# Hybrid RWKV-7 / MLA block on one core: a group's transposes in two steps on other PSUM banks, and two matmul orders turned round

## The chip, the cores and the metric

The kernel runs on one core of a Trainium2 chip. The time is device microseconds (us) of one execution on that core, compared by the median of several runs. The engines are TensorE (PE, with its weight loads PEld), VectorE (DVE), ScalarE (ACT), GpSimd (POOL) and SyncE (SP), which issues the DMAs here.

## The reference, cut to what matters

One layer over 256 latent and 256 context tokens of width 2048, all in float32. A combined input projection feeds a bidirectional RWKV-7 branch (16 heads of 64, two directions), a latent attention branch and gates; the branches are projected, merged and added to the stream.

```python
def rwkv7_step(S, xs):
    r, w, k, v, kk, akk = xs
    sa = jnp.einsum("dbhij,dbhj->dbhi", S, -kk)
    S = S * w[..., None, :] + sa[..., :, None] * akk[..., None, :] + v[..., :, None] * k[..., None, :]
    return S, jnp.einsum("dbhij,dbhj->dbhi", S, r)
...
S_ctx, y_c = rwkv_scan(r_c, v_c, kk_c, dec_c, a_c, km_c, S0)
_, y_x = rwkv_scan(r_x, v_x, kk_x, dec_x, a_x, km_x, S_ctx)
...
x_new = x + g_x * merge_branches(o_rw_x, o_ml_x, mg_x, w_branch_rwkv[i], w_branch_mla[i], w_out[i])
```

The scan over tokens is what the changed functions work on: the kernel does it in chunks of 64 tokens, with the values `v` and the keys of a chunk as matmul operands.

## The kernel before, in words

**Three terms for one product.** Most products are made with float32 operands split into a high and a low part, both read in a faster matmul form: `wh`, `wl` of a weight (ACT copies `wh` from the loaded `w`, DVE subtracts it to get `wl`, by `parts_of`) and `hmh`, `hml` of the activations. `mm3` issues three matmuls: wh with hmh, wh with hml, wl with hmh. PE's rows name the moving operand first, so they read `acc<-hmh,wh`, `acc<-hml,wh`, `acc<-hmh,wl`.

**Fill.** `proj_g` and `branch_g` make such products in bursts of twelve matmuls of 256 columns, or six of 512 columns, into the PSUM tiles named `acc`. `E.burst` keeps a burst together: its first matmul (its head, line L117 in the profile) is placed by ordinary priority, and the rest (L120) follow it by a high priority and an added dependency. Nothing in the scan waits soon for most of these bursts, so they are the work that is put between the steps of the scan. Here they are called fill.

**Groups of two halves.** A half is one pair of heads with one of the two token sets. Group k holds the latent half of pair k-1 (m = 0) and the context half of pair k (m = 1); the first and the last group hold one half. Four stretches of work follow one another for a group:

- `front` makes the decays, keys and products of each half (`wk<-Qc,BK` for context, `wk<-QR,BK` for latent) and starts `diagonal`, which inverts small blocks: the products go through DRAM (`dl`, `ln`), 28 small DVE operations work on `wt`, and the inverse comes back through DRAM (`dw`) as `WT`.
- `front2` transposes the values (two 128x128 transposes for a half, `wk<-cc,cv`, copied into `UV`) and the keys (eight for a half, `wk<-cc,BK`, copied by ACT into `BKT`). Each half takes three steps, so a full group takes six, all with the two PSUM buffers named `wk`.
- `back` begins with four levels (`lev`), 32 small matmuls each for a full group, into the two PSUM buffers named `lv`. Level 0 reads `WT` and `AQ`; the next three read `Z` or `ZN` with `WT`, `TF` or `W`. After each level DVE makes the next operand (`Z<-lv`, `W<-WT,lv`), one instruction for each half. In each pair of matmuls the latent one comes first. A level is a burst with two heads (four in level 0).
- Then `back` walks four chunks with three products each: `chp<-UV,AQ`, `chp<-xs,W`, `chp<-UV,BKT` (with `chp<-QR,Mn` and `chp<-AR,UV` for the latent outputs), each followed by a DVE or ACT copy that the next one reads.

**What sets the order.** `drive` writes the instructions down in Python from generators: at every `yield` of a chain it may put bursts of fill in between, by a model of time of its own. Conditions such as `yield lambda: backs >= k` hold a chain back. `bg_v(p)` (a value projection) becomes ready when the counter `fronts` passes a number. Then the scheduler of the tile framework orders the instructions of each engine by priority and by its own idea of when operands are there. The engines work through these orders as written.

The stages in time: the first projections to about 135 us, the scan with its fill to about 890 us, attention with fill to about 1117 us, then the last projections without fill.

## Time and profile before

| | |
|---|---|
| three runs | 1257.06, 1259.44, 1263.16 us (median 1259.44) |
| the profiled execution | 1256.53 us, of which its span is 1254.7 us |
| PE busy, share of the span | 1189.0 us, 95% |
| PEld, DVE, ACT busy | 1000.5 us (80%), 937.7 us (75%), 596.4 us (48%) |
| mean granted TensorE clock | 0.993 |
| chain that ended last | PE 70%, DMA 15%, DVE 11%, ACT 2% |

The span is what the instructions cover; the 1.8 us more in the execution's own time lie around it. PE is the engine to look at: it is idle for 66 us of the span, and only that idle time, and gaps between matmuls that the record counts as busy, can be gained or lost without a change in the work itself.

### The profile page before, as it was taken

How to read it: one execution, taken by the hardware profiler on the slowest of the kernel's cores; microseconds unless marked ns; L12 is line 12 of the kernel's file. 1: busy time of each engine (PE TensorE's matmuls, PEld its weight loads, DVE VectorE, ACT ScalarE, POOL GpSimd, SP SyncE). 2: the span in 40 equal slices, each digit the busy share in tenths (PEclk: the TensorE clock that was granted, in tenths of full speed). 3: DMA queues.
4: the chain of work that ended last, by engine and by line, in shares of the span. 5: the costliest groups of instructions: out<-in, count | busy, mean ns of one | idle time of the engine just before them, and what ended most of it. 6: DMA issues, size and time to landing. Idle time of an engine off the chain costs nothing.

```text
span 1254.7 us, 30101 instructions
## 1 busy us (share of the span) xinstructions
PE 1189.0 (95%) x11613; PEld 1000.5 (80%) x11613; DVE 937.7 (75%) x2642; ACT 596.4 (48%) x1244; POOL 1.9 (0%) x9
## 2 busy tenths in 40 slices
PE   5999998998999999999999899899999999899998
PEld 2665787787877777878887789789899999899886
DVE  4444767868888788888998888865877777768655
ACT  3444542444453454434544456344565656535443
POOL 0000000000000000000000000000000000000000
PEclk9999899999999999999999999999999999999999
DMA  9999447655554455544662655444855433689774
GB/s 377 347 351 352 144 122 180 163 156 146 128 154 126 119 139 136 148 117 124 167 151 62 162 157 146 127 114 142 255 181 152 138 109 115 193 283 295 220 254 139
DMA packets 214127, 222.53 MB, mean 177 GB/s; under 512 B 113168, under 2 KB 138400, under 8 KB 213472
## 3 DMA queue, kind: packets, MB, share of 16 engines
q1 hardware_dynamic: 213984, 220.61, 59.1%
q8 instruction: 91, 1.49, 0.5%
q14 instruction: 52, 0.43, 0.1%
HBM read 201.52 MB, written 19.03 MB: 176 GB/s over the span
## 4 chain that ended last, share of the span: by engine, by line
PE 70%; DMA 15%; DVE 11%; issue 2%; ACT 2%; SPq 0%; DVEq 0%; ACTq 0%
PE acc L120 29%; PE chp L115 11%; PE lv L115 6%; PE acc L117 5%; DMA wm<-in_w_mod_ss 4%; PE a L115 4%; PE ch L115 3%; DMA w<-in_w_proj 3%; DVE wl L142 3%; PE wk L115 2%; PE wk L127 2%; DMA ln<-dl 2%; PE wk L120 2%; PE acc L115 1%; DVE wt L142 1%
## 5 line engine op out<-in xcount | busy, mean ns | idle before, releaser
L142 ACT CAST wh<-w 128x512 fp32r<-128x512 f32 (+1 forms) x484 | 291.0, 608 | 328.4 <-PE acc L120 128.5
L142 DVE TENSOR_TENSOR wl<-w,wh 128x512 fp32r<-128x512 f32 (+1 forms) x480 | 322.6, 675 | 149.6 <-ACT wh L142 77.4
L120 PE MATMUL acc<-hmh,wl 128*128 128x256 f32 (+1 forms) x1312 | 396.7, 302 | 3.9 <-DVE wl L142 3.7
L120 PE MATMUL acc<-hml,wh 128*128 128x256 f32 (+1 forms) x1312 | 394.7, 301 | 0.0
L120 PE MATMUL acc<-hmh,wh 128*128 128x256 f32 (+1 forms) x928 | 273.8, 295 | 0.0
L120 PEld LDWEIGHTS acc<-hmh,wl 128*128 128x128 f32 x1312 | 248.8, 190 | 18.0 <-DVE wl L142 7.0
L120 PEld LDWEIGHTS acc<-hml,wh 128*128 128x128 f32 x1312 | 249.5, 190 | 8.8 <-issue 1.0
L120 PEld LDWEIGHTS acc<-hmh,wh 128*128 128x128 f32 x928 | 176.2, 190 | 5.0
L117 PE MATMUL acc<-hmh,wh 128*128 128x256 f32 (+1 forms) x384 | 146.6, 382 | 7.0 <-DVE th L142 3.5
L117 PEld LDWEIGHTS acc<-hmh,wh 128*128 128x128 f32 x384 | 72.8, 190 | 33.1 <-issue 15.1
L142 DVE TENSOR_TENSOR pr<-wt 64x14 f32<-64x14 f32 (+6 forms) x224 | 42.5, 190 | 2.6
L142 DVE TENSOR_TENSOR wt<-wt,pr 64x14 f32<-64x14 f32 (+6 forms) x224 | 42.3, 189 | 2.2
L115 PE MATMUL a<-hmh,wh 128*128 128x512 f32 x96 | 41.2, 429 | 0.0
L115 PE MATMUL a<-hmh,wl 128*128 128x512 f32 x96 | 38.6, 402 | 0.4 <-DVE wl L142 0.4
L115 PE MATMUL pm<-wm,ssil 128*32 128x256 f32 x512 | 34.5, 386 | 4.4 <-DMA wm<-in_w_mod_ss 4.2
L115 PE MATMUL a<-hml,wh 128*128 128x512 f32 x96 | 38.4, 400 | 0.0
L115 PE MATMUL chp<-obh,wl 128*128 128x256 f32 x128 | 36.2, 283 | 0.0
L115 PE MATMUL chp<-obl,wh 128*128 128x256 f32 x128 | 36.2, 283 | 0.0
L115 PE MATMUL chp<-obh,wh 128*128 128x256 f32 x128 | 36.2, 283 | 0.0
L142 ACT ACTIVATE hx<-hx,mod 128x256 f32<-128x256 f32 x32 | 17.5, 594 | 37.8 <-DVE mod L142 37.8
L142 DVE TENSOR_TENSOR hml<-hx,hmh 128x512 fp32r<-128x512 f32 x16 | 11.1, 693 | 29.0 <-ACT hmh L142 29.0
L115 PEld LDWEIGHTS pm<-wm,ssil 128*32 128x32 f32 x512 | 13.4, 109 | 23.3 <-DMA wm<-in_w_mod_ss 11.5
(347 smaller groups left out, 2223.6 us busy)
## 6 DMA issues: line engine op xcount, KB each, us to landing
w<-in_w_proj SPq DMA_DIRECT2D x296, 256.0 KB, 3.1
wm<-in_w_mod_ss SPq DMA_DIRECT2D x64, 512.0 KB, 7.5
w<-in_w_mod_g SPq DMA_DIRECT2D x64, 256.0 KB, 3.4
w<-in_w_br SPq DMA_DIRECT2D x64, 256.0 KB, 3.9
w<-in_w_out SPq DMA_DIRECT2D x64, 256.0 KB, 3.5
WT<-dw SPq DMA_DIRECT2D x32, 256.0 KB, 4.8
w<-in_w_first SPq DMA_DIRECT2D x32, 192.0 KB, 4.9
thd<-th SPq DMA_DIRECT2D x48, 128.0 KB, 2.9
```

The costliest lines, as they stand in the source:

```text
L115: return self.engine.matmul(out, lhsT=lhsT, rhs=rhs, **kw)
L117: self.head.append(self.engine.matmul(out, lhsT=lhsT, rhs=rhs, **kw))
L120: i = self.engine.matmul(out, lhsT=lhsT, rhs=rhs, **kw)
L127: return self.engine.transpose(*a)
L142: return fn(out, *a, **kw)
```

## The change

Four edits in one:

- `front2` takes all halves of a group at once. The values of both are transposed into one `wk` buffer (four transposes), then the keys of the first half into two `lv` buffers (eight transposes); the copies into `UV` come after. A second step transposes the keys of the second half. It waits for the values of both pairs, and `fronts` is raised by two at the end.
- `mm3w` takes the place of `mm3` in `proj_g` and `branch_g`: wl with hmh first, then wh with hmh, then wh with hml.
- In `lev` the two matmuls of a pair change places: context (m = 1) first, then latent.
- The steps of `front2` are two for a full group instead of six, which moves where `drive` puts fill.

```diff
+    def mm3w(ps, ah, al, bh, bl, start, stop):
+        E.matmul(ps, lhsT=al, rhs=bh, start=start, stop=False)
+        E.matmul(ps, lhsT=ah, rhs=bh, start=False, stop=False)
+        E.matmul(ps, lhsT=ah, rhs=bl, start=False, stop=stop)
...
-                            mm3(ps[:, 0:n], wh[:, cs], wl[:, cs], hmh[:, kk, 0:n], hml[:, kk, 0:n], kk == 0, kk == KT - 1)
+                            mm3w(ps[:, 0:n], wh[:, cs], wl[:, cs], hmh[:, kk, 0:n], hml[:, kk, 0:n], kk == 0, kk == KT - 1)
...
-        def front2(h, m, UV):
...
+        def front2(hs_, UV):
             ps = wk()
+            for m, h in enumerate(hs_):
+                t0 = 0 if h % 2 else T
+                for i in range(2):
+                    c0 = T * m + 128 * i
+                    E.transpose(ps[:, c0:c0 + 128], cvs_[h // 2][:, t0 + 128 * i:t0 + 128 * i + 128], ident)
+            def keys(h):
+                Q, AQ, AR, BK = halves[h]
+                BKT = rw.tile([P, 8, P], F32, name="BKT", bufs=2)
+                for i in range(2):
+                    pt = lvp()
+                    for j in range(4):
+                        E.transpose(pt[:, 128 * j:128 * j + 128], BK[:, 4 * i + j].rearrange("p a t -> p (a t)"), ident)
+                    S.copy(BKT[:, 4 * i:4 * i + 4].rearrange("p a t -> p (a t)"), pt)
+                halves[h] = (Q, AQ, AR, BKT)
+            keys(hs_[0])
...
+                        copies[b](UV6[hss[1 - g], g, :, :, b], src)
             yield
+            for h in hs_[1:]:
+                keys(h)
                 yield
...
-                            for t, fn, out in zip(ps, fns, outs):
+                            for t, fn, out in list(zip(ps, fns, outs))[::-1]:
...
-                for m, h in enumerate(hs_):
-                    yield lambda: h // 2 in cvs_
-                    yield from front2(h, m, UV)
-                    fronts += 1
+                yield lambda: hs_[-1] // 2 in cvs_
+                yield from front2(hs_, UV)
+                fronts += len(hs_)
...
-                        mm3(ps[:, 0:T], wh[:, cs], wl[:, cs], *(t[:, 4 * i + k] for t in ob[0]), i + k == 0, i * 4 + k == 7)
+                        mm3w(ps[:, 0:T], wh[:, cs], wl[:, cs], *(t[:, 4 * i + k] for t in ob[0]), i + k == 0, i * 4 + k == 7)
```

How the instructions move is seen in PE's order, in group 6's stretch of the scan. First the transposes of the keys, before: four of them stand alone between parts of the scan and a burst of fill.

```order
L115 MATMUL chp<-xs,W_8045 64x64 x4
L127 MATMUL wk<-cc,BK 128x128 x4
L115 MATMUL chp<-AR,UV 64x64
L117 MATMUL acc<-hmh,wh 128x512
L120 MATMUL acc<-hml,wh 128x512
L120 MATMUL acc<-hmh,wl 128x512
L120 MATMUL acc<-hmh,wh 128x512
L120 MATMUL acc<-hml,wh 128x512
L120 MATMUL acc<-hmh,wl 128x512
L115 MATMUL chp<-UV,BKT 64x64 x4
L115 MATMUL chp<-AR,UV 64x64 x3
L127 MATMUL wk<-cc,BK 128x128 x4
```

And PE after, the keys of the second half, eight in a row, with the end of one burst ahead and the head of the next behind (`acc<-w,ssil` are small gate matmuls):

```order
L120 MATMUL acc<-hmh,wh 128x256
L120 MATMUL acc<-hml,wh 128x256
L127 MATMUL lv<-cc,BK 128x128 x8
L115 MATMUL chp<-y,cc 128x256
L115 MATMUL acc<-w,ssil 32x256 x4
L117 MATMUL acc<-hmh,wl 128x256
L120 MATMUL acc<-hmh,wh 128x256
L120 MATMUL acc<-hml,wh 128x256
```

The transposes have gone into `lv`, in runs of eight instead of four, and the burst's head is now the product with `wl`.

Next PE at the start of level 1 of the same group, before. `lv<-WT_1361,Z` is the latent head; the context head `lv<-TF,Z` stands twelve rows of fill behind it.

```order
L120 MATMUL acc<-hml,wh 128x256
L120 MATMUL acc<-hmh,wl 128x256
L117 MATMUL lv<-WT_1361,Z 64x64
L117 MATMUL acc<-hmh,wh 128x256
L120 MATMUL acc<-hml,wh 128x256
L120 MATMUL acc<-hmh,wl 128x256
```

PE at the same place after:

```order
L120 MATMUL acc<-hml,wh 128x256
L117 MATMUL lv<-TF,Z 64x64
L117 MATMUL lv<-WT_1361,Z 64x64
L120 MATMUL lv<-TF,Z 64x64
L120 MATMUL lv<-WT_1361,Z 64x64
```

Both heads now stand together, and the level follows them without fill in between.

Last PE from the third level after level 0 to the first product that reads its result, `chp<-xs,W`, before (`wk<-kms,cc` belongs to another output):

```order
L117 MATMUL lv<-W_9203,Z 64x64 x2
L120 MATMUL lv<-W_9203,Z 64x64 x30
L115 MATMUL wk<-kms,cc 128x256
L115 MATMUL acc<-w,ssil 32x256
L115 MATMUL chp<-xs,W_9203 64x64 x2
L115 MATMUL chp<-QR,Mn 64x64 x2
L115 MATMUL chp<-xs,W_9203 64x64 x2
L115 MATMUL chp<-QR,Mn 64x64 x2
L115 MATMUL acc<-w,ssil 32x256 x3
```

And PE after, from the same level on:

```order
L117 MATMUL lv<-W_9323,Z 64x64 x2
L120 MATMUL lv<-W_9323,Z 64x64 x30
L117 MATMUL acc<-hmh,wl 128x512
L120 MATMUL acc<-hmh,wh 128x512
L120 MATMUL acc<-hml,wh 128x512
L120 MATMUL acc<-hmh,wl 128x512
L120 MATMUL acc<-hmh,wh 128x512
L120 MATMUL acc<-hml,wh 128x512
L115 MATMUL chp<-UV,AQ 64x64 x8
L115 MATMUL wk<-kms,cc 128x256
L115 MATMUL wk<-cc,gacc 128x2 x2
L117 MATMUL acc<-hmh,wl 128x512
```

A burst, the first product of the chunk and two small products now stand between the level and `chp<-xs,W`, which comes only after the burst that begins in the last row.

Counted over PE's whole order, from the first fill after the first projections to the last product of the scan: runs of like instructions 581 before, 533 after; among them runs of fill 209 and 192, runs of level matmuls 54 and 44, runs of key transposes 32 and 18, of value transposes 16 and 9. Fill inside the scan grows by 72 matmuls of 256 columns and falls by as many behind it; behind the last attention product 204 fill matmuls are left before and 180 after. In the stretch from the context products `wk<-Qc,BK` to that group's level 0, fill (in matmuls of 256 columns, one of 512 counted as two) goes from 204, 204, 216, 228, 216, 192, 204 in groups 1 to 7 to 276, 192, 156, 192, 180, 180, 204. From the end of level 0 to the last `chp<-UV,AQ` it goes from 204, 192, 144, 156, 156, 180 in groups 1 to 6 to 216, 264, 240, 240, 228, 252.

## The prediction

> **What bounds the kernel now.** I read the page's engine line first, then busy time by stage, then who PE waited for.

> ```profile
> PE 1189.0 (95%) x11613; PEld 1000.5 (80%) x11613; DVE 937.7 (75%) x2642; ACT 596.4 (48%) x1244; POOL 1.9 (0%) x9
> ```

> The scan and what is behind it: length, busy us of PE, PEld, DVE, ACT and POOL, granted clock, DMA share, GB/s.

> ```profile
> 135.00:890.00 755.00, 718.55 (x8358) 605.39 (x8356) 619.34 (x1870) 350.23 (x756) 1.53 (x4) 0.99 0.53 141
> 890.00:1254.00 364.00, 353.67 (x2390) 323.70 (x2389) 259.50 (x600) 190.71 (x377) 0.00 (x0) 1.00 0.61 194
> ```

> PE is the bound, at a granted clock of 0.99 to 1.00 in the two stages shown. The change issues the same matmuls, copies and DMAs as before in another order, so it can only touch PE's idle time and the gaps between unlike matmuls that the record counts as busy. The scan, 135 to 890 us, is where it acts: PE is idle there for 755 - 718.55 = 36.5 us. The first stage is not touched; behind the scan are 10.3 us of idle time. What ended PE's idle time in the scan, the largest rows and two smaller ones:

> ```profile
> engine line waited for: us in total, times, longest us
> PE lv L117 <- DVE W L142: 5.6, 11, 1.0
> PE chp L115 <- DVE xs L142: 5.0, 4, 2.0
> PE chp L115 <- DVE UV L142: 4.3, 7, 1.8
> PE wk L117 <- DVE QR L142: 4.0, 5, 1.4
> PE acc L120 <- DVE wl L142: 3.4, 9, 0.8
> PE acc L117 <- ACT wh L142: 2.7, 3, 1.5
> PE wk L127 <- DVE rnb L142: 2.1, 2, 1.9
> PE chp L115 <- DVE W L142: 1.7, 3, 1.2
> PE lv L117 <- DVE Z L142: 1.3, 3, 0.6
> ...
> PE chp L115 <- ACT UV L142: 1.1, 2, 0.8
> ...
> PE wk L127 <- ACT BKT L142: 0.4, 1, 0.4
> ```

> Read by edit: the levels and the chunk products (`lv` and `chp` rows) wait 5.6 + 5.0 + 4.3 + 1.7 + 1.3 + 1.1 = 19.0 us for operands that DVE or ACT makes from the step just before. Fill waits for its weights 6.1 us. The transposes themselves wait only 0.4 us. So "two steps, not six" wins almost nothing where it is made; what it does to the fill between other steps decides.

> **The change, part by part.** *Fewer switches between fill and the scan.* PE's rows around one switch, start and duration in us:

> ```profile
> 690.95 0.40 PE L120 MATMUL acc<-hml,wh 128*128 128x512 f32 x1
> 691.19 0.39 PE L120 MATMUL acc<-hmh,wl 128*128 128x512 f32 x1
> 691.51 0.64 PE L115 MATMUL acc<-w,ssil 128*32 128x256 f32 x8
> 692.08 0.39 PE L117 MATMUL acc<-hmh,wh 128*128 128x256 f32 x1
> 692.31 0.28 PE L120 MATMUL acc<-hml,wh 128*128 128x256 f32 x1
> ...
> 693.47 0.28 PE L120 MATMUL acc<-hmh,wl 128*128 128x256 f32 x1
> ```

> Starts of like matmuls lie 0.24 us apart at 512 columns and (693.47 - 692.31) / 10 = 0.116 at 256, which the counts below take as 0.117 (0.233 at 512). Leaving fill took 691.51 - 691.19 = 0.32, that is 0.08 more; the head after small matmuls took 0.23 to the next start, 0.11 more. So a run of fill costs 0.19 us. The order has 17 fewer of them: -3.2 us. Ends: 0, if what follows was waiting anyway, and -9.1, if each of the 48 runs that vanish (of any kind) is worth 0.19. I take the value that has rows.

> [...]

> *More cover between the steps of `back`.* Group 6 shows what a thin place costs:

> ```profile
> 712.24 0.22 PE L120 MATMUL lv<-W,ZN 64*64 64x64 f32 x1
> 712.39 0.69 PE L115 MATMUL chp<-UV,AQ 128*64 128x64 f32 x16
> ...
> 715.63 0.32 PE L117 MATMUL lv<-W,Z 64*64 64x64 f32 x2 [0.95 <-DVE W L142]
> 716.32 0.27 PE L117 MATMUL lv<-W,Z 64*64 64x64 f32 x1 [0.37 <-DVE W L142]
> ...
> 717.40 0.70 PE L115 MATMUL wk<-kms,cc 128*128 128x256 f32 x2
> ...
> 719.83 0.27 PE L115 MATMUL chp<-xs,W 64*64 64x64 f32 x2 [1.18 <-DVE W L142]
> ```

> From the end of a level (712.46) to the next one's first head PE needs 715.63 - 712.46 = 3.2 us, and to the second 3.9; one chunk product and one burst of twelve (in the place of the dots) cover it, and 0.95 + 0.37 us are lost. From the row behind that level (717.40) to `chp<-xs,W` it is 2.4 us, and 1.18 are lost: 2.5 us in one group. In the new order the first place has two bursts of six 512-column matmuls, 12 x 0.233 = 2.8 us, and the second two such bursts and three small products. Over the scan, fill from level 0 to the last chunk grows by 12, 72, 96, 84, 72 and 72 matmuls in groups 1 to 6, 1.4 to 11.2 us each at 0.117. The two heads of a level standing together belong here: the latent one no longer starts alone and is parted from the rest by a burst. Ends: 0, where the added fill lies at steps that were covered already, and -19.0, all these waits. Half, -9.5: the places that I can follow in group 6 lose nearly all of theirs, but with waits of 0.3 to 1.2 us each many will only shrink.

> *Less cover for the inverse.* The fill that moved came from between a group's products and its level 0, where the inverse goes through DRAM:

> ```profile
> 663.94 1.73 PE L120 MATMUL wk<-Qc,BK 64*128 64x64 f32 x28
> 676.77 0.17 DVE L142 TENSOR_TENSOR pr<-wt 64x14 f32<-64x14 f32 x1
> ...
> 690.73 0.14 DVE L142 TENSOR_TENSOR wt<-wt,pr 64x14 f32<-64x14 f32 x1
> 701.66 0.62 ACT L142 COPY TF<-WT 64x512 f32<-64x512 f32 x1 [1.19 <-DMA WT<-dw]
> 703.09 0.27 PE L117 MATMUL lv<-WT,AQ 64*64 64x64 f32 x1
> ```

> The products end at 665.67, `WT` has landed at 701.66 (ACT starts on it at once), and the level runs at 703.09: 36.0 us, and 1.4 us of slack. Fill in this stretch falls by 12, 60, 36, 36 and 12 matmuls in groups 2 to 6: 1.4, 7.0, 4.2, 4.2 and 1.4 us. Were nothing else to move, PE would stand at level 0 for what exceeds the slack: 0 + 5.6 + 2.8 + 2.8 + 0 = 11.2 us. But the inverse gets faster too. Its DVE part took 14.1 us here for 66 instructions from the first to the last of the `wt` work, foreign ones between included: 0.21 us each. The new order has 17, 18, 6, 13 and 14 foreign ones fewer in groups 2 to 6, so `WT` lands 3.6, 3.8, 1.3, 2.7 and 2.9 us earlier. What is left is 1.8 + 1.5 + 0.1 = +3.4 us. Ends: 0 and +18.3 (156 matmuls at 0.117, with the slack gone).

> *Low part first.* The head now needs `wl`, which DVE makes behind `wh`. Where PE waited for `wl`, 9 times and 3.4 us in all, two matmuls had already run; now they stand behind the wait. That adds two starts of 0.117 at each: 9 x 0.23 = +2.1 us. Ends: -3.4, if the order now has other work at these places, and +4.2, with 512-column matmuls. Queued behind the waiting head are the burst and whatever the scan has next on PE.

> *The banks, the copies, the values.* Moving the keys to `lv` gives back the 0.4 us for `BKT`. In exchange level 0 needs ACT's copy (0.59 us) out of these banks first; 72 or more fill matmuls, 8.4 us, stand between in groups 1 to 7, and 12, 1.4 us, in the last, so it is covered; without cover it would be 0.6 us a group. The copies into `UV` and `BKT` are as many as before. Waiting for both pairs' values costs nothing while `bg_v`, 48 matmuls of 512 columns (11.2 us), is fill that runs a group ahead (a group is about 82 us); if it came late, a group would lose up to these 11.2. SP has no DMA moved past another that PE waits for in the list above.

> **Sum.** -3.2 - 9.5 + 3.4 + 2.1 - 0.4 = -7.6 us. The profiled execution took 1256.53 us (span 1254.7), which makes 1248.9; it lies 2.9 below the median of the three runs, 1259.44, and against the median I forecast 1251.8, 0.6% faster.

> **The rivals.**
> *The waits only move* (chance 0.18). If the fill added in `back` stands at covered steps, or the waits come back where fill was taken away, in the fronts (`wk<-QR` has 4.0 us already) or in attention, the 9.5 is 0: -3.2 + 3.4 + 2.1 - 0.4 = +1.9, 1261. For it: fill is only moved, 72 matmuls, 8.4 us, out of the stages behind. Against it: 180 fill matmuls are still left behind the last attention product, so attention does not run dry.
> *Switches cost nothing* (0.06): the weights of the head load under the small matmuls and its longer record is only latency. Then -4.4, 1255.0. The starts quoted speak against it. [...]
> *Level 0 comes before `WT`* (0.16). If DVE is no quicker with `wt` (it is 619.34 of 755 us busy, so its order is not all that delays it), PE stands at level 0 in groups 2 to 6, up to 18.3 us: -3.2 - 9.5 + 18.3 + 2.1 - 0.4 = +7.3, 1266.7. It decides from 11.0 us of such waits on, where the sum is zero. For it: ACT waited for this DMA in this group, and the slack was 1.4. Against it: the DVE order between first and last is shorter in every group from 2 on.

> **How the numbers follow.** The forecast has 0.60, with a range of its own from 1243 to 1256; 0.10 of it falls within 0.5% of 1259.4 (6.3 us, about what a measurement of this kernel can tell from no change). So faster 0.50, same 0.10 + 0.18 + 0.06 = 0.34, slower 0.16. Adding the favourable ends gives -9.1 - 19.0 - 3.4 - 0.4 = -31.9 and the bad ones 18.3 + 4.2 = +22.5, but they need all terms at once; the range 1243 to 1263 leaves about 0.08 below it and 0.12 above, where the last rival stands.

> **What would show it.** Right: PE's waits for `W`, `Z`, `xs` and `UV` in the scan sum to about 10 us instead of 19.0; PE's idle time there is below 36.5; level heads stand in pairs. The inverse: a row in which `lv<-WT` waits for the DMA, a few us in all. Low part first: the wait for `wl` moves from L120 to L117 and is 5 to 6 us. Wrong: waits at `lv<-WT,AQ` above 11 us, the six chain waits still near 19, or idle time behind 890 us grown past 10.3 by as much as the scan gained.

## The result, and the profile after

The changed kernel took 1269.08 us (median of 7 runs, 1264.29 to 1271.38) beside 1257.7 for the kernel before on the same chip (7 runs): 1.008 times its time, 95% interval 1.0054 to 1.0107. It is slower by 0.8%; the forecast was 0.6% faster, with 0.16 on slower. Its profiled execution took 1264.29 us (span 1262.5, against 1254.7). The engine line, then the stretches that answer to those of before (length, busy us of PE, PEld, DVE, ACT and POOL, granted clock, DMA share, GB/s):

```profile
PE 1183.3 (94%) x11613; PEld 997.2 (79%) x11613; DVE 941.7 (75%) x2642; ACT 593.4 (47%) x1244; POOL 1.9 (0%) x9
```

```profile
135.00:890.00 755.00, 704.45 (x8278) 594.25 (x8278) 613.59 (x1824) 342.31 (x748) 0.24 (x2) 0.99 0.52 138
890.00:1262.00 372.00, 360.60 (x2465) 330.82 (x2463) 267.84 (x644) 194.20 (x383) 0.21 (x1) 1.00 0.62 195
```

PE was busy 5.7 us less (1189.0 to 1183.3) and idle 13.5 us more (65.7 to 79.2). The idle time grew in the scan, from 36.5 to 755 - 704.45 = 50.6 us; behind it it went from 10.3 to 11.4. What ended PE's idle time between 135 and 898 us, the largest rows (the last scan product, `chp<-AR,UV`, ends at 887.3 us instead of 868.6; 72 more fill matmuls, 8.4 us at 0.117 each, stand ahead of it):

```profile
PE acc L117 <- DVE wl L142: 16.5, 19, 2.7
PE wk L117 <- DVE QR L142: 5.7, 6, 2.1
PE lv L117 <- DVE W L142: 4.9, 7, 1.4
PE chp L115 <- DVE xs L142: 4.2, 4, 2.1
PE chp L115 <- DVE UV L142: 3.7, 4, 1.2
PE wk L127 <- DVE rnb L142: 3.5, 3, 2.7
PE wk L117 <- DVE AR L142: 3.3, 4, 1.1
PE lv L117 <- DVE wt L142: 2.6, 1, 2.6
PE chp L127 <- DVE rvb L142: 2.1, 3, 1.8
...
PE lv L127 <- ACT BKT L142: 0.7, 1, 0.7
...
PE chp L115 <- ACT UV L142: 0.3, 1, 0.3
```

The chain waits (`W`, `Z`, `xs`, `UV`) fell from 19.0 to 4.9 + 4.2 + 3.7 + 0.3 = 13.1 us, as meant. In the same stretch fill's waits for its own weights rose from 7.1 to 16.5 us, all of them now at the head of a burst. Before, three of the rows were:

```profile
PE acc L120 <- DVE wl L142: 3.7, 10, 0.8
PE acc L117 <- ACT wh L142: 3.4, 4, 1.5
PE wk L117 <- DVE AR L142: 1.1, 3, 0.5
```

A third part grew as well: `QR`, `AR` and `rnb` (the keys' preparation and the fronts) went from 4.0 + 1.1 + 2.1 = 7.2 to 5.7 + 3.3 + 3.5 = 12.5 us, `wt` at level 0 from nothing to 2.6 and `rvb` from 0.8 to 2.1. So of the 13.0 us that the idle time of this stretch grew by (37.6 to 50.6), the chain is -5.9, fill +9.4 and everything else +9.5. One waiting head in the timeline: rows of PE, then DVE, ACT and SP's queue (start, duration, in brackets the idle time before and what ended it):

```profile
711.12 0.64 PE L115 MATMUL acc<-w,ssil 128*32 128x256 f32 x8
713.84 0.39 PE L117 MATMUL acc<-hmh,wl 128*128 128x256 f32 x1 [2.07 <-DVE wl L142]
...
708.78 0.68 DVE L142 TENSOR_TENSOR wl<-w,wh 128x512 fp32r<-128x512 f32 x1
...
713.09 0.69 DVE L142 TENSOR_TENSOR wl<-w,wh 128x512 fp32r<-128x512 f32 x1 [0.48 <-ACT wh L142]
...
712.44 1.24 ACT L142 CAST wh<-w 128x512 fp32r<-128x512 f32 x2 [2.77 <-DMA w<-in_w_proj]
...
706.92 1.74 SPq L907 DMA_DIRECT2D dw<-wt  x2
708.70 1.25 SPq L237 DMA_DIRECT2D w<-in_w_proj  x2
```

PE waits for `wl`, DVE waits for `wh`, ACT waits for the load, and the load was issued at 708.70, behind the inverse's stores in SP's queue (`dw<-wt`). Fill's weights come out of a loop: a load buffer is free when DVE has made `wl` from it, then SP issues the next load, ACT makes `wh`, DVE makes `wl`. What SP's queue waited for most in the scan is the first of these links (195.0 us before, so it did not grow):

```profile
SPq L237 <- DVE wl L142: 191.0, 103, 8.0
```

### The profile page after: what moved, and what is told of

It reads as the page before. It is cut to its first block, busy times and chain, and to the rows that moved or that the text cites. A ratio compares the mean times of both kernels' runs of the same rounds, so it can differ in the third digit from the quotient of the medians.

```text
span 1262.5 us, 30074 instructions
## 1 busy us (share of the span) xinstructions
PE 1183.3 (94%) x11613; PEld 997.2 (79%) x11613; DVE 941.7 (75%) x2642; ACT 593.4 (47%) x1244; POOL 1.9 (0%) x9
## 5 line engine op out<-in xcount | busy, mean ns | idle before, releaser
L142 ACT CAST wh<-w 128x512 fp32r<-128x512 f32 (+1 forms) x484 | 290.2, 607 | 339.7 <-PE acc L120 141.7
L142 DVE TENSOR_TENSOR wl<-w,wh 128x512 fp32r<-128x512 f32 (+1 forms) x480 | 321.7, 674 | 133.2 <-ACT wh L142 72.4
L120 PE MATMUL acc<-hmh,wh 128*128 128x256 f32 (+1 forms) x1312 | 394.2, 300 | 0.0
L120 PE MATMUL acc<-hml,wh 128*128 128x256 f32 (+1 forms) x1312 | 393.6, 300 | 0.0
L120 PE MATMUL acc<-hmh,wl 128*128 128x256 f32 (+1 forms) x928 | 273.5, 295 | 0.0
L120 PEld LDWEIGHTS acc<-hml,wh 128*128 128x128 f32 x1312 | 248.3, 189 | 10.3
L120 PEld LDWEIGHTS acc<-hmh,wh 128*128 128x128 f32 x1312 | 248.9, 190 | 8.7 <-ACT wh L142 0.7
L120 PEld LDWEIGHTS acc<-hmh,wl 128*128 128x128 f32 x928 | 175.7, 189 | 5.0
L117 PE MATMUL acc<-hmh,wl 128*128 128x256 f32 (+1 forms) x384 | 146.4, 381 | 22.6 <-DVE wl L142 18.6
L117 PEld LDWEIGHTS acc<-hmh,wl 128*128 128x128 f32 x384 | 72.6, 189 | 52.1 <-DVE wl L142 27.1
L142 DVE TENSOR_TENSOR pr<-wt 64x14 f32<-64x14 f32 (+6 forms) x224 | 42.5, 190 | 3.5
L142 DVE TENSOR_TENSOR wt<-wt,pr 64x14 f32<-64x14 f32 (+6 forms) x224 | 42.4, 189 | 3.6
L115 PE MATMUL a<-hmh,wh 128*128 128x512 f32 x96 | 40.7, 424 | 0.0
L115 PE MATMUL pm<-wm,ssil 128*32 128x256 f32 x512 | 35.3, 394 | 4.1 <-DMA wm<-in_w_mod_ss 3.9
L115 PE MATMUL a<-hmh,wl 128*128 128x512 f32 x96 | 37.9, 395 | 0.3 <-DVE wl L142 0.3
L115 PE MATMUL a<-hml,wh 128*128 128x512 f32 x96 | 37.9, 395 | 0.0
L115 PE MATMUL chp<-obh,wl 128*128 128x256 f32 x128 | 36.2, 283 | 0.0
L115 PE MATMUL chp<-obl,wh 128*128 128x256 f32 x128 | 36.2, 283 | 0.0
L115 PE MATMUL chp<-obh,wh 128*128 128x256 f32 x128 | 36.2, 283 | 0.0
L142 ACT ACTIVATE hx<-hx,mod 128x256 f32<-128x256 f32 x32 | 17.5, 595 | 38.0 <-DVE mod L142 38.0
L142 DVE TENSOR_TENSOR hml<-hx,hmh 128x512 fp32r<-128x512 f32 x16 | 11.1, 693 | 29.0 <-ACT hmh L142 29.0
L115 PEld LDWEIGHTS pm<-wm,ssil 128*32 128x32 f32 x512 | 13.8, 111 | 22.9 <-DMA wm<-in_w_mod_ss 10.4
```

The source lines that it names most:

```text
L115: return self.engine.matmul(out, lhsT=lhsT, rhs=rhs, **kw)
L117: self.head.append(self.engine.matmul(out, lhsT=lhsT, rhs=rhs, **kw))
L120: i = self.engine.matmul(out, lhsT=lhsT, rhs=rhs, **kw)
L142: return fn(out, *a, **kw)
```

## The experiments

Each was timed in five rounds against the kernel before on the same chip (its medians there were 1260.71 us beside x1 to x4, 1260.56 beside x5 to x8, 1261.56 beside x9 to x12, 1264.35 beside x13 to x15 and 1260.43 beside x16 to x18). The table gives the ratio with its interval and, of the profiled execution, four sums in us: PE's idle time; PE's busy time that was lost at half clock (an estimate: half of what it was busy in stretches with a granted clock of 0.5; last section); PE's busy time without that; and the waits of the chain and of fill between 135 and 898 us, added up from the list of waits by the names used above. The four sums are of one execution each: in the first row its granted clock was 0.993, while 35 executions of the kernel before average 0.9891, so its half-clock column is, by estimate, about 5 us lower than usual (0.0039 of 1257).

| kernel | ratio | idle | half clock | rest of PE | chain | fill |
|---|---|---|---|---|---|---|
| before | 1 | 65.7 | 8.2 | 1180.8 | 19.0 | 7.1 |
| after | 1.0080 [1.0054, 1.0107] | 79.2 | 11.0 | 1172.3 | 13.1 | 16.5 |
| x1 two steps, levels | 1.0033 [1.0014, 1.0053] | 75.9 | 8.4 | 1176.6 | 13.9 | 17.0 |
| x2 low first | 1.0061 [1.0038, 1.0084] | 71.9 | 14.6 | 1178.5 | 17.7 | 10.2 |
| x3 level order | 0.9992 [0.9969, 1.0015] | 70.1 | 20.3 | 1174.8 | 18.5 | 6.3 |
| x4 two steps | 1.0046 [1.0023, 1.0069] | 72.4 | 8.6 | 1179.8 | 10.5 | 16.0 |
| x5 low last | 1.0019 [0.9996, 1.0041] | 69.0 | 14.7 | 1176.7 | 17.6 | 4.1 |
| x6 x1, low last | 1.0048 [1.0029, 1.0066] | 76.5 | 12.3 | 1171.9 | 13.7 | 15.9 |
| x7 two steps, wk banks | 1.0108 [1.0083, 1.0132] | 68.9 | 21.4 | 1179.7 | 12.1 | 10.7 |
| x8 six steps, lv banks | 1.0075 [1.0047, 1.0103] | 69.0 | 21.1 | 1180.5 | 17.1 | 7.8 |
| x13 after, more fill ahead | 1.0148 [1.0103, 1.0193] | 81.2 | 13.6 | 1181.6 | 10.5 | 14.5 |
| x16 before, double bursts | 1.0249 [1.0216, 1.0282] | 85.2 | 30.6 | 1177.5 | 14.3 | 9.7 |
| x17 x1, half bursts | 1.0122 [1.0082, 1.0162] | 69.5 | 13.2 | 1188.3 | 11.3 | 7.9 |
| x18 before, half bursts | 1.0123 [1.0088, 1.0157] | 64.8 | 15.3 | 1189.3 | 6.2 | 11.0 |

The ratios of the runs that are not in the table stand with them below.

### The parts alone

Two steps and level order, without low-first (`mm3w` back to `mm3` in both places of the changed kernel):

> The changed kernel with the three terms of a fill product in the old order (wh with hmh first). Theory A, the low part at the head: PE's waits of L117 for wl (18.6 us in all after the change) go, waits for wl and wh in fill fall back to about 6 us, and the time is 8 to 13 us below the changed kernel, so 0 to 4 us below the one before. Rival B, the two steps and the level order cost by what they do to the scan's order (QR, AR and rnb waits): the time stays within 4 us of the changed kernel. Rival C, any new order of this program moves it by several us: the time comes out anywhere between, and the waits change in rows that the edit does not touch.

Low-first alone (in the kernel before):

```diff
-    mm3(ps[:, 0:n], wh[:, cs], wl[:, cs], ...)
+    mm3w(ps[:, 0:n], wh[:, cs], wl[:, cs], ...)
```

> The kernel before with only the low part first in the fill products. Theory A: 8 to 13 us slower than before, with 10 us or more of PE waiting at L117 for wl. Rival B: within 3 us of before, waits for wl about 6 us. Rival C: any number between, with the difference spread over rows of the scan.

The level order alone:

```diff
-    for t, fn, out in zip(ps, fns, outs):
+    for t, fn, out in list(zip(ps, fns, outs))[::-1]:
```

> The kernel before with only the context matmul first in each pair of a level. By the forecast: isolated level heads go, 5 to 10 runs fewer on PE, 1 to 4 us faster. Theory A says nothing against that. Rival C: up to 6 us either way.

Two steps alone (`front2` and its call from the changed kernel, nothing else):

> The kernel before with only the transposes of a group in two steps and the keys in the levels' banks. By the forecast: fewer runs of fill, more fill in the levels and chunks, 2 to 6 us faster. Rival B: 4 to 10 us slower, with PE waiting in the fronts (QR, AR, rnb) and at level 0. Rival C: up to 6 us either way.

Measured: 1265.96, 1268.97, 1261.45 and 1266.03 us. Low-first costs 0.61%, the two steps 0.46%, the level order nothing; the first two add up to a little more than the 0.80% of the whole. x1 lies between its first two theories, x2 at the lower edge of the range of theory A; the gains forecast for x3 and x4 did not come, and x4 lies in the range of its rival B, but with its new waits at fill more than in the fronts. PE's waits in the kernel with two steps alone, 135 to 898 us:

```profile
PE acc L120 <- DVE wl L142: 9.2, 25, 1.0
PE lv L117 <- DVE W L142: 6.9, 9, 1.9
PE acc L117 <- ACT wh L142: 6.8, 10, 1.7
PE wk L117 <- DVE QR L142: 5.0, 4, 1.4
...
PE chp L115 <- DVE UV L142: 1.8, 2, 1.4
PE chp L115 <- DVE xs L142: 1.8, 2, 1.3
```

The chain waits fell by 8.5 us (19.0 to 10.5), close to the 9.5 forecast, and fill's waits rose by 8.9 (9.2 + 6.8 = 16.0 from 7.1). The two sums together are 26.1 before and 26.5 here: the waits moved from the steps to the fill put between them. Idle time in the scan is 38.7 us, against 37.6; the other 5.6 us of the 6.7 that came stand outside it, 4.3 of them behind 898 us (9.9 to 14.2). So the moved waits show why the scan won nothing; what made this run slower lies mostly behind it, and no run follows that up.

### Where the wl matmuls stand

All matmuls that read `wl` at the end of the burst, in the kernel before (x5) and with two steps and level order (x6):

The edit in short:

```diff
-    for k in ks: mm3(...)        # wh.hmh, wh.hml, wl.hmh for each k
+    for k in ks: wh.hmh, wh.hml
+    for k in ks: wl.hmh
```

> The kernel before, with all matmuls of a fill burst that read wl moved behind all that read wh; nothing else is changed. It is the mirror of low-first. Theory (the wait for wl at a burst's head is what low-first costs, and the later wl is needed the less it costs): the waits on wl in the scan, 3.4 us in the kernel before, fall under 1 us; wh's 2.7 us stay; PE idle in the scan 36.5 -> 33 to 35; 0 to 4 us faster than before. Rival (low-first costs through the weight order itself, for instance because matmuls of one weight tile no longer stand together): here they do not stand together either, the time is 2 to 8 us above before. Rival (any changed order moves the time by some us): slower or faster with no link to wl.

> Two steps for values and keys in the levels' banks, levels with context first, and the matmuls on wl at the end of each burst (in the place of low part first). Theory (the two steps push fill against a DVE with no idle time ahead of level 0, so its weights come late): the waits for wl, 13.0 us in the scan with the two steps and the level order, fall by half or more as each burst needs wl eight matmuls later; wh's 6.3 stay or grow by some us, since DVE holds up ACT as well; about 3 us less than the two steps and level order together, 1260 to 1264. If the waits only turn into waits on wh, 1265 to 1267. Rival (the cost is not fill's weights but the two steps' own place in the order): 1265 to 1267 with wl waits gone.

In x5 the wait for `wl` went as expected, and nothing was won. In x6 it turned into a wait for `wh`, and the time stayed at 1266.82. The rows of fill in the list of waits of x5:

```profile
PE acc L117 <- ACT wh L142: 3.8, 3, 1.7
...
PE acc L120 <- DVE wl L142: 0.3, 2, 0.2
```

and of x6:

```profile
PE acc L117 <- ACT wh L142: 12.4, 10, 2.5
...
PE acc L120 <- DVE wl L142: 3.5, 6, 0.8
```

So in the kernels with two steps the order of the three matmuls mostly chooses which of the two operands is waited for: the sum is 17.0 us in x1, 15.9 in x6 and 16.5 in the changed kernel.

### Steps or banks

Two steps with the keys in `wk` banks (x7); six steps with the keys in `lv` banks (x8):

```diff
-                    pt = lvp()        # x7, from two steps alone
+                    pt = wk()
...
-                ps = wk()             # x8, from the kernel before
+                ps = lvp()
```

> Two steps for values and keys, but the keys' transposes in the wk banks as before, not in the levels'. Theory (the number of steps, so the fill's place, makes the cost): 1264 to 1268, as with both. Rival (the levels' banks make it: a level waits for the copies out of them): 1259 to 1262, the fill's waits back at 6 to 9 us.

> The kernel before, with only the keys' transposes in the levels' banks; six steps as before. Theory (steps, not banks): 1258 to 1262, no change, and fill's waits for wl and wh near 6 us. Rival (banks): 1264 to 1268.

1274.09 and 1270.3 us: neither bank change is free, and both lie above the ranges of their two theories. In the profiled executions the two lose little by idle time (68.9 and 69.0), but 13 us more each at half clock. Over all their executions the clock explains less: 0.9823 and 0.9845 on average against 0.9895 for the kernel before on that chip, which by estimate (0.0072 and 0.0050 of their times) is about 9 and 6 of the 13.6 and 9.5 us. The line of span and granted clock of x7 (0.993 before):

```profile
core 0: 1269.9 us, clock 0.982
```

and of x8:

```profile
core 0: 1270.6 us, clock 0.982
```

### Without the work on the low parts

Both kernels make `wl` from the first piece of each width alone and use it for all later pieces, so they leave out the low parts of all other weights:

```diff
-            split(w, h, l)
+            S.copy(h, w)
+            if key not in lows:       # key: pool and width
+                lows[key] = ...; V.tensor_tensor(lows[key], w, h, ALU.subtract)
```

> The changed kernel, but wl is made only from the first piece of each width and kept; all later pieces use it, so DVE no longer makes the 0.68 us wl of each piece. This leaves out the low parts of all other weights; PE's matmuls, their order and the loads stay. Theory (the two steps and low-first lose by the wl that DVE makes late ahead of level 0): PE's waits for wl, 16.5 us in the scan, go to 0, wh's rise by 2 to 5 us at most, PE idle in the scan falls from 50.6 to about 35; and against the kernel before with the same edit this one is 2 to 8 us faster, since what the change gains in chain waits (about 6 us) and PE's busy time (about 6 us) stays. Rival (the new order costs by itself, through waits elsewhere): it stays 5 to 10 us above the kernel before with the same edit.

> The kernel before with the same edit: wl made only from the first piece of each width and kept, which leaves out the low parts of all other weights. Control for the run above. Theory: wl's 3.4 us of waits go to 0 and some waits of the chain for DVE shrink as DVE has about 0.68 us less for each piece: 3 to 12 us faster than the kernel before.

1247.79 us (0.9897 [0.9874, 0.9921]) and 1232.46 us (0.9759 [0.9734, 0.9783]). Both are faster, x10 by 29 us where 3 to 12 were expected. x9 lies 15 us above x10; my theory that `wl` alone eats the gain had it 2 to 8 us below, and it fell. PE's waits in the changed kernel with this edit (the four rows in which the levels wait for the inverse or for `En`, and fill's):

```profile
PE lv L117 <- DVE pr L142: 7.3, 4, 5.3
PE acc L120 <- ACT wh L142: 3.8, 2, 2.5
...
PE lv L117 <- DVE wt L142: 2.8, 2, 1.5
...
PE lv L117 <- DMA WT<-dw: 2.3, 1, 2.3
PE lv L117 <- ACT En L142: 2.0, 1, 2.0
```

and the largest in the kernel before with it:

```profile
PE lv L117 <- DVE W L142: 12.5, 8, 2.7
PE wk L117 <- DVE QR L142: 7.0, 5, 2.2
PE acc L117 <- ACT wh L142: 1.5, 3, 1.0
```

Fill waits little (3.8 and 1.5 us), and in the changed kernel PE then waits at the levels for the inverse: 7.3 + 2.8 + 2.3 us, and 2.0 for `En`: 14.4 us, where x10 has 1.0. Three things limit the reading. The edit also shortens the loop of loads: a load buffer is now free when ACT has made `wh`, as SP's largest wait in x9 shows, so DVE's time and the loop's length are not told apart.

```profile
SPq L238 <- ACT wh L142: 247.8, 152, 5.9
```

The planner and the scheduler put fill elsewhere when DVE has less to do, so the two programs differ from their originals by more than the edit; and the profiled execution of x9 is the slowest of its seven (1257.71).

### Three wl buffers for one load buffer

```diff
-NW, NSP, NSL = 4, 3, 2
+NW, NSP, NSL = 3, 3, 3
```

> The changed kernel with three buffers for wl instead of two, paid for with three buffers for loaded pieces instead of four. Theory (fill asks for a wl each 1.4 us, and two buffers bridge 2.8 us while DVE's latent front lasts 3 to 4): a third bridges 4.2 us, the waits for wl fall from 16.5 to 4 to 10 us, and the time to 1260 to 1265. If DVE is simply short of time there, whatever the buffers: no change, 1266 to 1270. If three loaded pieces are too few, PE or ACT wait for DMA, and the next kernel shows it too.

> The kernel before with the same buffers: three for wl, three for loaded pieces. Control: wl's 3.4 us go under 2, and 1257 to 1262 if the loads don't mind; 1264 or more if they do.

1325.75 (1.0491 [1.0454, 1.0529]) and 1319.8 us (1.0455 [1.0426, 1.0483]). As a test of the third buffer it is worthless, since the control lost as much. But it shows how tight the loop of loads is: with one load buffer of four fewer, and one for `wl` more, both kernels lose about 60 us, and fill's waits up to 898 us are 26.6 and 19.4 us.

### More fill ahead of level 0

In the 22 us ahead of level 0, summed over the groups from the second on, PE is idle for about 7 us before and for 14 to 15.5 in x1, x4, x6, x7 and the changed kernel. The order of the changed kernel has 18 us less fill between products and level 0 in groups 2 to 6.

```diff
-LT = (3.5, 5.0, 2.0, 4.5, 5.5)
+LT = (3.5, 5.0, 2.0, 4.5, 9.5)
```

> The changed kernel with one number of the order's planner changed: the time it allows for the last transfer of the inverse is 9.5 instead of 5.5 us, so it sets level 0 later and more fill ahead of it: 28 us on average between a group's products and level 0 in groups 2 to 7, instead of 21. Two theories of why PE is idle for 15.0 us (instead of 7.3) in the 22 us ahead of the levels. Cover: the two steps took 18 us of fill out of this place, and the inverse is as slow as before; put back, the idle time there falls to 7 to 10 us and the time to 1260 to 1266. Supply: DVE, 88% busy there, can't make wl for more fill; the idle time stays at 13 to 18 us, the stretch gets longer, and the time is 1267 to 1276.

> Two steps and level order, high part first as before the change, with the same number at 9.5. Cover: idle ahead of level 0 from 14.6 to 7 to 10 us, time 1256 to 1262, at or below the kernel before. Supply: idle stays, 1264 to 1272.

> The kernel before with the same number at 9.5. Control: fill ahead of level 0 hardly changes (25.2 us a group instead of 24.5), so both theories expect 1258 to 1266.

1281.63, 1287.92 (1.019 [1.0149, 1.023]) and 1267.46 us (1.0032 [1.0004, 1.006]). The idle time ahead of level 0 fell to 4.9 us in x13 and to 7.7 in x14, as cover said; but both times lie above the ranges of both theories, and x15's just above its own. In x13 the way from products to level 0 grew from 36 to 48 us a group, fill's waits for `wl` were still 14.5 us, and idle time in all was 81.2, with 20.2 us of it behind 898 us instead of 11.9. Giving the fill back moved the waits again and cost 0.7% more.

### Longer and shorter runs of fill

```diff
-                    yield             # x16: after every second 256-column piece only
+                    if n > T or i:
+                        yield
...
-                for ks in ((0, 1), (2, 3)) if n > T else ((0, 1, 2, 3),):    # x17, x18
+                for ks in ((0, 1), (2, 3)):
```

> The kernel before, six steps, high part first, but the 256-column fill hands control back after every second piece, so it comes 24 matmuls at a time instead of 12: 2044 fill matmuls of the scan's order stand in runs of 24 or more, instead of 870 (1124 to 1302 in the kernels with two steps and the levels' banks). Theory (bunched fill asks for weights faster than DVE and ACT make them): the waits of fill for wl and wh, 7 us in the scan, rise to 15 to 25 us, 5 to 15 us slower. Rival (the place of the fill, not its bunching): the waits stay under 10 us, and the time within 4 us.

> Two steps and level order, but the 256-column fill hands control back after each half piece, 6 matmuls: 742 fill matmuls in runs of 24 or more instead of 1196, and 26 fill runs more. Bunching: the waits for wl and wh fall from 19.3 us to 6 to 12, PE's busy time grows by about 26 x 0.19 = 5 us: 1258 to 1264, below the 1266 of the two. Rival (place, or DVE's work whatever the order): waits stay above 15, 1266 to 1274.

> The kernel before with half pieces: 638 fill matmuls in runs of 24 or more instead of 870, 34 fill runs more. Control: waits for wl and wh from 7 to 2 to 5 us, PE's busy time up by about 34 x 0.19 = 6 us: 1258 to 1267.

1291.68, 1276.1 and 1275.59 us, all above the ranges that were forecast. x17 brought fill's waits from 17.0 to 7.9 us as bunching said; but PE's idle time between 135 and 898 us did not follow (42.7 to 46.2), since other rows grew, and its fall in all, from 75.9 to 69.5, stands behind the scan. And 26 more runs of fill cost 1188.3 - 1176.6 = 11.7 us of PE's own time, 0.45 each, and in x18 34 runs cost 8.5, 0.25 each. x16 and x18 speak against bunching as the whole cause: runs twice as long left fill's waits at 9.7 us, and in x18, where shorter runs were to bring them to 2 to 5 us, they rose from 7.1 to 11.0. The 31 us of x16 went elsewhere: in its profiled execution idle time grew by 19.5 us, most of it behind the scan, and 22.4 us more were lost at half clock.

## Why the prediction was wrong

*The step that failed* is "More cover between the steps of back": it took the chain's waits as won (-9.5) and gave the fill that covers them a price of zero beyond PE's own time. The chain waits did fall, by 8.5 us with the two steps alone and by 5.9 in the whole. But fill is not free cover: each 12 matmuls need a new `wh` and `wl` from the same ACT and DVE that the chain waits for, and those waits rose by 8.9 us (x4). It is close to the rival "The waits only move" (0.18): between 135 and 898 us PE's idle time is 37 to 40 us in nine kernels (before, x3, x4, x5, x7, x8, x15, x16 and x18), though the chain's share ranges from 6.2 to 19.0. In the others that compute the whole reference, x11 and x12 aside, the waits grew: to 42.7 in x1, 42.9 in x2, 44.3 in x6, 42.7 in x13, 45.2 in x14, 46.2 in x17 and 50.6 in the changed kernel, so moving is not all. Where DVE lost work it fell, to 28.2 from 37.6 (x10) and to 41.9 from 50.6 (x9). That rival had the waits come back in the fronts or in attention: in the changed kernel `QR`, `AR` and `rnb` took 5.3 us more, fill's weights, which it did not name, 9.4. And it gave 1261; x4 measured 1266.03. And "SP has no DMA moved past another" looked at moves alone: fill's loads already stand behind the inverse's stores in SP's queue, as at 708.70.

*Low part first*, +2.1 with an end of +4.2, measured +0.61%, 7.7 us (x2). Fill's waits, in its profiled execution, explain 3.1 of it. The granted clock explains, by estimate, about 3.4: over its 12 runs it is 0.9864 on average (the changed kernel's 7 runs give the same), and 0.9891 over the 35 of the kernel before; 0.0027 of 1265 us is 3.4. The rest is in other rows; the largest new one is a single wait of 3.5 us of the gate matmuls for a load. The list had the wait moving from L120 to L117 at 5 to 6 us; it did move, and is 16.5. On top of the two steps and the level order, low-first leaves fill's waits where they were (17.0 in x1), but the idle time between 135 and 898 us goes from 42.7 to 50.6: it came in the rows `QR`, `AR`, `rnb`, `wt` and `rvb`.

*Fewer switches*, -3.2 for 17 runs, was right in sign: PE's time outside the half-clock stretches fell from 1180.8 to 1172.3, 8.5 us, with 18 runs fewer over the whole order (260 and 242). That the runs alone made this is not shown. x17 and x18 put a run at 0.45 and 0.25 us instead of 0.19, but x4 has 6 runs more and 1.0 us less, x3 5 fewer and 6.0 less, x13 10 fewer and 0.8 more. The rival that switches cost nothing is hard to hold beside x17 and x18. No run shows what in a switch costs, the weight loads or something else.

*Less cover for the inverse*, +3.4: level 0 itself waited 2.6 us for `wt` once and never for `WT`, so the third rival did not come in that form. But DVE's part of the inverse did not become 1.3 to 3.8 us shorter throughout: from the first to the last `wt` operation it takes 13.5 us on average over groups 2 to 7 before and 12.9 after, though a fifth fewer instructions stand between. In groups 2, 3 and 5 it is 2.8 to 3.5 us shorter, about as forecast; in groups 4 and 6 it is 3.1 and 1.6 us longer. PE's idle time in the 22 us ahead of level 0 grew mostly at fill (1.0 to 8.0 us at `wl`) and not at the level itself.

*The level order, the banks, the copies*: the order of the two matmuls of a pair is worth nothing measurable (0.9992), though that may be two effects that cancel: PE's time without half clock is 6.0 us lower in x3, and its clock, 0.9872 on average, costs about 2.4 by the same estimate. I gave the banks a gain of 0.4 us; alone they cost 0.75% (x8), while with two steps `lv` banks (x4) are faster than `wk` banks (x7).

Of the 7.8 us between the two spans, idle time is +13.5, half clock +2.8 and the rest of PE -8.5. My sum had idle time at -9.5 + 3.4 + 2.1 - 0.4 = -4.4 and PE at -3.2. It had no term for the granted clock, since I took PE's idle time and the gaps between matmuls for all that an order can change; the half-clock stretches are a third thing.

Still open: why the same fill waits more for its weights when the keys and values take two steps. Its place (x13) and the length of its runs (x16) each failed as the only cause; that its loads, `wh` and `wl` stand in queues behind the inverse's work at that time is seen in rows such as those above, and was not isolated. Open too is why `QR`, `AR` and `rnb` are waited for longer in the changed kernel. No version that computes the whole reference was measurably faster than the kernel before.

## What to carry to other kernels

Work that is put under a wait has a supply of its own: before fill counts as cover, ask which engine and which buffer make its operands, and whether that engine is the one that is late. When the sum of waits stays the same while their names change, as here in nine kernels of one family, a better order is unlikely to win; look at the work of the engine that most of the waits name. Here that was DVE, and the only two kernels that were faster had less work on it, though they also had a shorter loop of loads. And a wait of PE can cost more than its own length: here the window of 3.41 us behind one in which PE was busy for less than 1.5 us was at half clock 77 times of 77, which by estimate takes up to 1.7 us more.

## What the runs showed of the hardware

```profile
398.70:402.10 3.40, 2.18 (x37) 1.91 (x35) 3.09 (x12) 1.81 (x5) 0.00 (x0) 1.00 0.67 222
402.10:405.50 3.40, 3.40 (x17) 3.40 (x18) 2.24 (x10) 1.49 (x3) 0.00 (x0) 0.50 0.29 77
716.20:719.60 3.40, 1.75 (x24) 1.48 (x24) 3.37 (x9) 0.72 (x1) 0.00 (x0) 0.99 0.57 192
719.60:723.00 3.40, 3.40 (x72) 3.06 (x69) 3.40 (x13) 3.19 (x6) 0.00 (x0) 0.51 0.43 105
```

The grid of 3.41 us was laid over all 20 traces, from 130 us on. Where PE was busy for less than 1.5 us of a window, the next was at half clock 77 times of 77; from 1.5 to 2.0 us, 57 of 107; from 2 to 3 us, 49 of 669; above 3 us, 14 of 5795. Each costs by estimate up to 1.7 us, half of 3.41, where PE is busy all through it, as in the two above; fill matmuls of 256 columns start 0.213 us apart in the one at 402.10 and 0.117 behind it (405.58 to 406.40). The kernel before had 5 such windows in its profiled execution, the changed kernel 7, and x16, with this line, 22:

```profile
core 0: 1293.3 us, clock 0.971
```

Ahead of the two above PE was not idle all through: it was busy for 2.18 and 1.75 us of 3.40.
